# Hybrid decoder block: written instruction order replaced by list scheduling on four engines in the input projection

## The chip, the cores and the metric

The kernel runs on one core of a Trainium2 chip. A core has five engines with instruction streams of their own: TensorE (PE, matmuls and transposes, with its weight loads listed apart as PEld), VectorE (DVE), ScalarE (ACT), GpSimd (POOL) and SyncE (SP, which here only issues DMAs). Each engine works through its own list of instructions; between engines, semaphores make one wait for another. The metric is the device time of one execution in microseconds (us).

## The reference

One layer of a decoder on 2048 positions of width 1024, all in float32. The input projection is the part that this change touches:

```python
mod = silu(c) @ w_ada + b_ada                  # shift, scale, gate for mixer and FFN
h = rms_norm(x) * (1 + scale1) + shift1
p = h @ w_in                                   # (2048, 3088), split into the columns of three groups
q_a, k_a, v_a = ...                            # attention, 8 heads x 64; q_a, k_a are rms-normed per head
q_m, k_m, v_m, o_m, i_m, f_m = ...             # mLSTM, 4 heads x 64, chunk recurrence over 64 positions
u_s, v_s = ...                                 # spatial gating, 4 groups x 64, chunks of 128 positions
y = concat(attention, sigmoid(o_m) * rms_norm(mlstm), gelu(u_s) * spatial(layer_norm(gelu(v_s)))) @ w_out
x = x + gate1 * y
x = x + gate2 * conv_ffn(rms_norm(x) * (1 + scale2) + shift2)
```

## The kernel before

Each float32 matrix product is done as three matmuls on two halves of each operand (`mm3`, L53 to L56): a high part (`hh` of h, `wh` of the weight) and the rest (`hl`, `wl`); the product of the two rests is left out. PE has three places for a product in progress (`acc`), two of them in the last V step.

The projection takes about the first 770 us. It runs in 14 steps (`steps`, L1136): a half of the positions (eight row tiles of 128) times a block of weight columns. Blocks are KM with the gates (272 columns), QO (512, transposed output), VM (256), U and S of the gating (512), K, Q and V (512 each). A row tile of a step is 24 matmuls, 8 slices of 128 in depth (k) times three, into one `acc`; then it is evicted by ACT and DVE. K and Q tiles are normed on the way: ACT squares (`qsq`, L836), DVE sums (`ss`, L841, L842), POOL takes the power -1/2 (L128), DVE multiplies (`qn`, L846), PE transposes (L850), and ACT and DVE split the result into `qhi` and `qlo` (L854, L855), which SP writes to `q_d` or `k_d` (L857). V tiles go through `vhl` (L829, L830) to `v_d` (L831).

Between the tiles side work is interleaved. `slot()` (L463) is called after a tile (and within some), and lets each waiting "lane", a Python generator, do one piece: the weight loads `wr` (L632, L640) and casts `wh` (ACT, L652) and `wl` (DVE, L653) of the next step, which `products` (L682) spreads over the tiles; the rest of the modulation (`wa` loads L486, multiplications L500 and L502 into `modacc`, the bias row L517, the sum over partitions on PE L521 or L527); the mLSTM chunks and, at each quarter's end, `mlstm_end` (L1067) with its sum L1082, L1083, the power on POOL L1084 and the product L1086; norm and transposes of the next rows of x (L559 to L571, L605, L609 to L611, where `xt` is a normed row tile); and in the last step the first rows of scores (L206 to L223) of attention head 0, with their loads of `kk`, `nf` and `q` (L157, L158, L173).

The framework has two ways to order instructions. By default a list scheduler puts each engine's instructions into an order of its own making, from its model of their durations and their dependencies. Inside `tc.manual_schedule(engines=...)` the named engines keep the order in which the Python code writes the instructions. The first step (`first_block`, L1146) is outside; steps 1 to 13 are inside, for PE, DVE, ACT and POOL. SP is never named, so the DMA issues are always ordered by the scheduler. Behind the projection both programs are the same.

Of the kernel before, what the change touches and what calls it, by code (L numbers as in the profile page):

```python
# [33 lines left out]
def trunk(  # L34
# [103 lines left out]
    def attention_open_right():  # L138
        pool.open("att_s", "right", ("nm", 8, 6), ("rs", 8, 6))
        pool.open("att_r", "right", ("kvA", 8192, 3), ("LA", 4096, 8), ("qA", 2048, 4))  # L140
        pp.open("att_r", "right", ("sp", 4096, 2))
# [9 lines left out]
    def load_k(h):  # L151
        tag, e = "kvA" if h == 0 else "kvB", slice(h % 2 * 64, h % 2 * 64 + 64)
        kk = pool.tile([P, S], F32R, name="kk", tag=tag)
        nf = pool.tile([P, S], F32, name="nf", tag=tag)
        vv = pool.tile([P, S // P, P], F32R, name="vv", tag=tag)
        for i in range(2):
            dma(kk[64 * i : 64 * i + 64].bitcast(F32), k_d[h // 2, i, e])  # L157
        dma(nf, nf_d[h : h + 1, :].broadcast_to([P, S]))  # L158
        kv[h] = kk, nf, vv

    def load_v(h, cs):
        for c in cs:
            dma(
                kv[h][2][:, 4 * c : 4 * c + 4].bitcast(F32),
                v_d[c * TB : (c + 1) * TB, h, :].rearrange("(n p) d -> p n d", p=P),
            )

    def load_q(h, tb, tag):
        q2 = []
        for n in range(2):  # L170
            t = pool.tile([P, TB], F32R, name="q", tag=tag)
            for i in range(2):
                dma(  # L173
                    t[64 * i : 64 * i + 64].bitcast(F32),
                    q_d[h // 2, n, h % 2 * 64 : h % 2 * 64 + 64, tb * TB : (tb + 1) * TB],
                )
            q2.append(t)
        return q2
# [281 lines left out]
    def lane(steps_, delay=1, own=False, heavy=False):  # L460
        lanes.append([now[0] + delay, steps_, own, heavy])

    def slot(busy=False, drain=False):  # L463
        now[0] += 1
        for ln in list(lanes):
            if drain and ln[2]:
                continue
            if ln[0] <= now[0] and not (busy and ln[3]):
                w = next(ln[1], 0)
                if w == 0:  # L470
                    lanes.remove(ln)
                else:
                    ln[0] = now[0] + (w or 1)
# [62 lines left out]
    def small_setup():  # L536
        rows = []
        for i in range(2):
            r = pool.tile([P, P], F32, name="crow", tag="tmpA")
            if i == 0:  # L540
                dma(r[0:44], w_conv[0, 0].rearrange("(k p) -> k p", p=P))
                dma(r[44:88], w_conv[0, 1].rearrange("(k p) -> k p", p=P))
            else:
                dma(r[0:44], w_conv[0, 2].rearrange("(k p) -> k p", p=P))
                dma(r[44:88], b_conv[0].rearrange("(k p) -> k p", p=P))
            rows.append(r)
        yield 3
        for i, r in enumerate(rows):
            ps = misc_ps()
            T.transpose(ps[:, 0:88], r[0:88, :], ident[0:88, 0:88])  # L550
            V.tensor_copy(colC[:, i * 88 : (i + 1) * 88], ps[:, 0:88])
            yield 1
# [312 lines left out]
    def log_gates():  # L865

        fox, fm = gates[:, :, 64:72], gates[:, :, 32:36]
        mn = pool.tile([P, 8, 12], F32, name="lg0", tag="lg")
        ab = pool.tile([P, 8, 12], F32, name="lg1", tag="lg")
        for sl, g in ((slice(0, 8), fox), (slice(8, 12), fm)):  # L870
            V.tensor_scalar(mn[:, :, sl], g, 0.0, None, op0=ALU.min)
            V.scalar_tensor_tensor(ab[:, :, sl], mn[:, :, sl], 2.0, g, op0=ALU.mult, op1=ALU.subtract)
        A.activation(ab, ab, AF.Exp)
        A.activation(ab, ab, AF.Ln, bias=1.0)
        yield 1
        for sl, g in ((slice(0, 8), fox), (slice(8, 12), fm)):
            V.tensor_tensor(g, mn[:, :, sl], ab[:, :, sl], op=ALU.subtract)
# [232 lines left out]
    def refill():  # L1110
        xs = [load_x(8 + t) for t in range(4)]
        yield 3
        yield from normed(xs)
        for k in range(KT):
            make_h(2, xs, (k,))
            if k not in (4, 6):
                yield 1
        xs = [load_x(12 + t) for t in range(4)]
        yield 4
        yield from normed(xs)  # L1120
        for k in range(0, KT, 2):
            make_h(3, xs, (k, k + 1))
            yield 1
# [60 lines left out]
    def in_turn(*gens):  # L1184
        for g_ in gens:
            yield from g_

    in_order = tc.manual_schedule(
        engines={mybir.EngineType.PE, mybir.EngineType.DVE, mybir.EngineType.Activation, mybir.EngineType.Pool}
    )  # L1190
    for n, (half, i) in enumerate(steps):
        if n == 1:
            in_order.__enter__()
            lane(in_turn(log_gates(), iter((6,)), small_setup()), 2)
            lane(rest_of_mod(), 1)
        if n == 3:
            lane(in_turn(mlstm(0, 2), mlstm(1, 7)), 2, False, True)
        if n == nb - 1:
            lane(refill(), 3)
        if n == nb + 2:  # L1200
            lane(in_turn(log_gates(), iter((1,)), mlstm(2, 1), mlstm(3, 1, 1)), 1, False, True)
        if n == len(steps) - 1:
            assert n_mod[0] == 64, n_mod
            while any(not ln[2] for ln in lanes):
                slot(drain=True)
            n_accs[0] = 2
            pool.close("proj_r")
            pp.close("proj_r")
            attention_open_right()

            load_k(0)
            first_rows = [], []
            first = [scores(0, tb, load_q(0, tb, "qA"), r) for tb, r in zip((1, 0), first_rows)]
            load_v(0, (0, 1))
            lane(in_turn(*first), 7, True)
        light[0] = 2 if n == 1 else int(0 < n and i < 3)
        if n in (1, nb):
            light[1] = now[0] + (23 if n == 1 else 31)
        nxt[0] = Weights(blocks[steps[n + 1][1]][0]) if n + 1 < len(steps) else None
        if n == 0:  # L1220
            first_block()
        else:
            blocks[i][1](half, cur)
        if nxt[0]:
            nxt[0].cast()
        cur = nxt[0]
    in_order.__exit__(None, None, None)
    pool.close("proj_l")
    pp.close("proj_l")

# [624 lines left out]
```

## Time and profile before

| | |
|---|---|
| three runs | 2670.3, 2672.68, 2673.54 us (median 2672.68) |
| profiled execution | 2675.71 us, of which 2674.0 are the span |
| mean granted PE clock of the profiled execution | 0.988 |
| busy: PE, PEld, DVE, ACT, POOL | 2580.6, 2128.9, 1992.1, 1285.4, 415.6 us |
| DMA | 377.52 MB, mean 141 GB/s |

The profile comes from one execution; its times start at the span's start. A row of the timeline gives the start, the busy time, the engine, the line, what is computed from what, and in brackets how long the engine had been idle and what it had been waiting for. The granted clock is the share of full speed that PE was allowed; below 1 every matmul takes longer. Names in the profile are without the numbers that tell the tiles apart; where a number is given below, it comes from the program's order.

### The profile page before, as it was taken

To read this page: it belongs to the slowest core of one execution; us is meant where nothing else is said; L and a number is where in the kernel's file an instruction comes from. 1 tells how busy PE (TensorE), PEld (TensorE's weight loads), DVE (VectorE), ACT (ScalarE), POOL (GpSimd) and SP (SyncE) were. 2 spreads that over 40 slices of the span, in tenths; PEclk is the share of its full clock that TensorE was granted. 3 is DMA by queue.
4 is the path that set the end of the run, shared out by engine and by line. 5 is a ranking of instruction groups with operands and counts; after the bars stand their busy time and mean duration, and the time that the engine had idled before them with its cause. 6 is when DMAs were issued, how large, how long until landed. Compare 5 with 4: busy or idle time off the path is not lost.

```text
span 2674.0 us, 36818 instructions
## 1 busy us (share of the span) xinstructions
PE 2580.6 (97%) x12761; PEld 2128.9 (80%) x12761; DVE 1992.1 (75%) x3432; ACT 1285.4 (48%) x2442; POOL 415.6 (16%) x550
## 2 busy tenths in 40 slices
PE   5899999999899999999999999999999999999999
PEld 5788787888777877777877888888888888888787
DVE  5555656455448888876749888887988887898797
ACT  3333334333248788874436544444444444444443
POOL 4012210022236566640000000000000000000000
PEclk9899999999999999999999999999999999999999
DMA  7533556424554444536742222228222225748533
GB/s 257 154 117 91 150 152 184 132 70 123 138 171 123 115 133 125 136 98 229 276 142 72 90 84 84 82 84 294 89 85 82 84 79 206 267 148 308 177 101 116
DMA packets 297683, 377.52 MB, mean 141 GB/s; under 512 B 31118, under 2 KB 189676, under 8 KB 295448
## 3 DMA queue, kind: packets, MB, share of 16 engines
q1 hardware_dynamic: 297496, 375.16, 44.4%
q8 instruction: 101, 1.65, 0.3%
q14 instruction: 86, 0.70, 0.1%
HBM read 274.34 MB, written 100.74 MB: 140 GB/s over the span
## 4 chain that ended last, share of the span: by engine, by line
PE 74%; DVE 11%; DMA 5%; ACT 4%; issue 4%; POOL 1%; SPq 0%; DVEq 0%; ACTq 0%; POOLq 0%
PE ub L54 10%; PE ub L56 10%; PE ub L55 10%; PE acc L54 5%; PE acc L56 5%; PE acc L55 5%; PE db L55 4%; PE db L56 4%; PE db L54 4%; PE tp L259 3%; PE sp L206 3%; PE op L245 2%; PE op L246 2%; DVE wspl L1599 2%; DMA x_d<-x 1%
## 5 line engine op out<-in xcount | busy, mean ns | idle before, releaser
L54 PE MATMUL acc<-wh,hh 128*128 128x512 f32 (+2 forms) x768 | 290.8, 379 | 10.9 <-DVE vhl L830 5.3
L55 PE MATMUL acc<-wl,hh 128*128 128x512 f32 (+2 forms) x768 | 277.5, 361 | 4.5 <-POOL wl L677 3.4
L54 PE MATMUL ub<-T,wsph 128*128 128x512 f32 x704 | 274.3, 390 | 5.8 <-ACT wsph L1467 5.8
L56 PE MATMUL acc<-wh,hl 128*128 128x512 f32 (+2 forms) x768 | 278.1, 362 | 0.4 <-DVE hl L611 0.4
L56 PE MATMUL ub<-T,wspl 128*128 128x512 f32 x704 | 273.8, 389 | 0.4 <-DVE wspl L1468 0.4
L55 PE MATMUL ub<-T,wsph 128*128 128x512 f32 x704 | 273.9, 389 | 0.0
L55 PE MATMUL db<-wspl,wsph 128*128 128x512 f32 x616 | 240.4, 390 | 2.2 <-DVE wspl L1599 2.2
L56 PE MATMUL db<-wsph,wspl 128*128 128x512 f32 x616 | 239.6, 389 | 0.0
L54 PE MATMUL db<-wsph 128*128 128x512 f32 x616 | 238.3, 389 | 0.3 <-ACT wsph L1598 0.3
L1467 ACT CAST wsph<-S 128x512 fp32r<-128x512 f32 x176 | 109.7, 623 | 228.6 <-PE ub L55 162.5
L263 DVE TENSOR_TENSOR plo<-tp,phi 128x512 fp32r<-128x512 f32 (+1 forms) x320 | 186.8, 607 | 35.9 <-ACT phi L262 34.0
L54 PE MATMUL ub<-B,wsph 128*128 128x512 f32 x528 | 207.3, 393 | 2.6 <-ACT wsph L1467 2.6
L56 PE MATMUL ub<-B,wspl 128*128 128x512 f32 x528 | 207.0, 392 | 0.8 <-DVE wspl L1468 0.8
L55 PE MATMUL ub<-B,wsph 128*128 128x512 f32 x528 | 207.1, 392 | 0.0
L223 ACT ACTIVATE L<-L,nm 128x1024 f32<-128x1024 f32 (+2 forms) x192 | 172.5, 902 | 32.1 <-DVE nm L212 30.8
L259 PE MATMUL tp<-ident,L 128*128 128x128 f32 x1088 | 178.6, 276 | 5.2 <-DVE vhl L830 1.9
L262 ACT CAST phi<-tp 128x512 fp32r<-128x512 f32 (+1 forms) x320 | 160.1, 521 | 46.0 <-PE tp L259 44.7
L54 PEld LDWEIGHTS acc<-wh,hh 128*128 128x128 f32 x768 | 148.3, 193 | 32.3 <-issue 6.6
L206 PE MATMUL sp<-kk,q 128*128 128x512 f32 (+3 forms) x640 | 168.4, 374 | 2.3 <-DVE nm L212 1.2
L228 POOL TENSOR_SCALAR L<-L,rs 128x1024 f32<-128x1024 f32 (+2 forms) x192 | 167.2, 881 | 11.2
L1598 ACT CAST wsph<-act 128x512 fp32r<-128x512 f32 x132 | 82.2, 623 | 179.0 <-PE db L55 162.6
L55 PEld LDWEIGHTS acc<-wl,hh 128*128 128x128 f32 x768 | 148.2, 193 | 25.1 <-POOL wl L677 3.7
(344 smaller groups left out, 6025.8 us busy)
## 6 DMA issues: line engine op xcount, KB each, us to landing
w<-in_w_up_dram SPq DMA_DIRECT2D x88, 512.0 KB
wd<-in_w_down_dram SPq DMA_DIRECT2D x176, 256.0 KB
wa<-in_w_ada_dram SPq DMA_DIRECT2D x96, 256.0 KB
act_d<-yc SPq DMA_DIRECT2D x44, 512.0 KB
act<-act_d SPq DMA_DIRECT2D x44, 512.0 KB
wr<-in_w_in_dram SPq DMA_DIRECT2D x76, 256.0 KB
q<-q_d SPq DMA_DIRECT2D x128, 128.0 KB
hc_d<-hl SPq DMA_DIRECT2D x28, 512.0 KB
```

The lines of the kernel that those rows point to most:

```text
L54: T.matmul(ps, lh, rh, start=start, stop=False, skip_group_check=resume)
L55: T.matmul(ps, lh, rl, start=False, stop=False, skip_group_check=resume)
L56: T.matmul(ps, ll, rh, start=False, stop=stop, skip_group_check=resume)
L206: T.matmul(sp[:, b : b + bw], q2[n][:, qs], kk[:, s0 + b : s0 + b + bw], start=n == 0, stop=n == 1 and not last)
L223: A.activation(L[c], L[c], AF.Exp, bias=nm[:, n - 1 : n], scale=-1.0, accum_out=rs[:, c : c + 1])
L228: G.tensor_scalar(t, t, rs[:, 0:1], 1.0, op0=ALU.mult, op1=ALU.mult)
L245: T.matmul(op[:, c0:], vv[:, j, :], hi[:, c0:], start=(j == 0), stop=False)
L259: T.transpose(tp[:, i * P : (i + 1) * P], rows[i][j // 8][:, (j % 8) * P : (j % 8 + 1) * P], ident)
L262: A.copy(hi[:, c0:], tp[:, c0:])
L263: V.tensor_tensor(lo[:, c0:], tp[:, c0:], hi[:, c0:].bitcast(F32), op=ALU.subtract)
L1467: A.copy(hi, src)
L1598: A.copy(hi, v)
```

## The change

The region in which four engines keep the written order is taken out. From step 1 on the list scheduler now orders PE, DVE, ACT and POOL too, together with the first block and with what follows. No instruction is added, removed or changed on any engine.

```diff
-    in_order = tc.manual_schedule(
-        engines={mybir.EngineType.PE, mybir.EngineType.DVE, mybir.EngineType.Activation, mybir.EngineType.Pool}
-    )
     for n, (half, i) in enumerate(steps):
         if n == 1:
-            in_order.__enter__()
             lane(in_turn(log_gates(), iter((6,)), small_setup()), 2)
             lane(rest_of_mod(), 1)
...
         if nxt[0]:
             nxt[0].cast()
         cur = nxt[0]
-    in_order.__exit__(None, None, None)
     pool.close("proj_l")
     pp.close("proj_l")
```

The order shows some 146 PE, 670 DVE, 79 ACT, 59 POOL and 270 SP instructions at other places, all in the first 780 us or so. Three places are shown. The tile numbers of the changed kernel are two lower, and lines behind L1188 four or five lower.

First, PE in the first block (about 67 to 80 us of the profile), where `trp` are the transposes of the second four row tiles `xt`, one `trp` for each slice k, and `acc_811` (now `acc_809`) is the first product that needs them. Before, the last transposes and the first matmuls behind them:

```order
L605 MATMUL trp_789<-ident_74,xt_570 128x128
L605 MATMUL trp_800<-ident_74,xt_564 128x128
L605 MATMUL trp_800<-ident_74,xt_566 128x128
L605 MATMUL trp_800<-ident_74,xt_568 128x128
L605 MATMUL trp_800<-ident_74,xt_570 128x128
L54 MATMUL acc_811<-wh_346,hh_729 128x272
L55 MATMUL acc_811<-wl_347,hh_729 128x272
L56 MATMUL acc_811<-wh_346,hl_730 128x272
```

And in the changed kernel, where the transposes of slice 2 and 3 begin:

```order
L605 MATMUL trp_743<-ident_74,xt_562 128x128
L605 MATMUL trp_743<-ident_74,xt_564 128x128
L605 MATMUL trp_743<-ident_74,xt_566 128x128
L605 MATMUL trp_743<-ident_74,xt_568 128x128
L54 MATMUL acc_809<-wh_346,hh_727 128x272
L55 MATMUL acc_809<-wl_347,hh_727 128x272
L605 MATMUL trp_754<-ident_74,xt_562 128x128
L605 MATMUL trp_754<-ident_74,xt_564 128x128
L605 MATMUL trp_754<-ident_74,xt_566 128x128
L605 MATMUL trp_754<-ident_74,xt_568 128x128
L56 MATMUL acc_809<-wh_346,hl_728 128x272
L54 MATMUL acc_846<-wh_346,hh_727 128x272
```

The matmuls of the first slices, of several products at once, moved in between the transposes of the later slices.

Second, DVE at the end of the first half's K step (about 287 to 299 us), where `wl` are the casts of the Q weights and H and `mss` belong to the end of an mLSTM quarter. Before:

```order
L1075 TENSOR_TENSOR H_1861<-H_1861,den_2701 128x16x64
L846 TENSOR_TENSOR qn_2712<-acc_2584,ss_2659 128x512
L653 TENSOR_TENSOR wl_2719<-wr_2556,wh_2718 128x512
L653 TENSOR_TENSOR wl_2728<-wr_2619,wh_2727 128x512
L653 TENSOR_TENSOR wl_2737<-wr_2681,wh_2736 128x512
L841 TENSOR_REDUCE ss_2743<-qsq_2675 128x8
L842 TENSOR_SCALAR ss_2743<-ss_2743 128x8
L653 TENSOR_TENSOR wl_2754<-wr_2722,wh_2753 128x512
L855 SCALAR_TENSOR_TENSOR qlo_2771<-trp_2765,colA_87,qhi_2770 128x512
L846 TENSOR_TENSOR qn_2776<-acc_2643,ss_2743 128x512
L653 TENSOR_TENSOR wl_2779<-wr_2731,wh_2778 128x512
```

And after:

```order
L653 TENSOR_TENSOR wl_2735<-wr_2679,wh_2734 128x512
L842 TENSOR_SCALAR ss_2741<-ss_2741 128x8
L941 TENSOR_TENSOR decr_2794<-mprev_2626,ra_2619 4x4
L943 SCALAR_TENSOR_TENSOR fr_2796<-ones_83,fc_1799,mps_2621 8x512
L846 TENSOR_TENSOR qn_2774<-acc_2641,ss_2741 128x512
L947 COPY fc_2798<-fr_2796 8x1
L1083 TENSOR_SCALAR mss_2803<-mss_2803 128x16
L927 COPY mprev_4854<-mcar_297 4x1
L1086 TENSOR_TENSOR hq_2708<-H_1859,mss_2803 128x1024
L653 TENSOR_TENSOR wl_2752<-wr_2720,wh_2751 128x512
L855 SCALAR_TENSOR_TENSOR qlo_2769<-trp_2763,colA_87,qhi_2768 128x512
L653 TENSOR_TENSOR wl_2777<-wr_2729,wh_2776 128x512
```

The two last casts, `wl_2752` and `wl_2777`, now stand behind L1083 and L1086, between which POOL's L1084 has to be done; `qn_2710` (before `qn_2712`) moved ahead of L1075, out of this piece.

Third, SP at the end of the projection (about 704 to 723 us): `wr` are the loads of the V weights, `kk`, `nf` and `q` the loads for the scores of head 0. Before:

```order
L857 DMA q_d_60<-qhi_6736 128x4x128
L640 DMA wr_6721<-in_w_in_dram 128x512
L1095 DMA yt_d_68<-yt_6728 128x512
L857 DMA q_d_60<-qlo_6737 128x4x128
L640 DMA wr_6752<-in_w_in_dram 128x512
L640 DMA wr_6761<-in_w_in_dram 128x512
L857 DMA q_d_60<-qhi_6800 128x4x128
L857 DMA q_d_60<-qlo_6801 128x4x128
L857 DMA q_d_60<-qhi_6867 128x4x128
L857 DMA q_d_60<-qlo_6868 128x4x128
L157 DMA kk_6829<-k_d_61 64x2048 x2
L158 DMA nf_6830<-nf_d_63 128x2048
```

And after:

```order
L857 DMA q_d_60<-qhi_6734 128x4x128
L1095 DMA yt_d_68<-yt_6726 128x512
L857 DMA q_d_60<-qlo_6735 128x4x128
L640 DMA wr_6750<-in_w_in_dram 128x512
L640 DMA wr_6759<-in_w_in_dram 128x512
L157 DMA kk_6827<-k_d_61 64x2048
L857 DMA q_d_60<-qhi_6798 128x4x128
L857 DMA q_d_60<-qlo_6799 128x4x128
L157 DMA kk_6827<-k_d_61 64x2048
L158 DMA nf_6828<-nf_d_63 128x2048
L173 DMA q_6833<-q_d_60 64x512 x2
L173 DMA q_6836<-q_d_60 64x512 x2
```

The load `wr_6719` (before `wr_6721`) is no longer in this piece; it is a dozen rows earlier. The loads of head 0 moved ahead of the last writes to `q_d` and of the writes of `vhl` to `v_d`. On PE the first six score rows of head 0 (L206, L210), which stood one by one between halves of the V products, are now one group ahead of `acc_6974`.

## Prediction

> **What bounds the kernel now.** I read the page's totals first, then the windows of 25 us, then the timeline of TensorE (PE), which puts the idle time before a group in brackets with what ended it.
>
> ```profile
> span 2674.0 us, 36818 instructions
> PE 2580.6 (97%) x12761; PEld 2128.9 (80%) x12761; DVE 1992.1 (75%) x3432; ACT 1285.4 (48%) x2442; POOL 415.6 (16%) x550
> PEclk9899999999999999999999999999999999999999
> ```
>
> PE is busy for 97% of the span, and both programs hold the same PE instructions. An order can therefore give or take only PE's idle time and time at a low granted clock. Both lie early:
>
> ```profile
> 50.00:75.00 25.00, 19.55 (x107) 17.14 (x106) 11.49 (x37) 12.22 (x28) 3.50 (x8) 0.77 0.28 95
> 100.00:125.00 25.00, 25.00 (x104) 20.48 (x104) 12.00 (x20) 6.80 (x9) 0.00 (x0) 0.90 0.76 232
> 275.00:300.00 25.00, 21.49 (x93) 16.63 (x92) 18.50 (x33) 10.62 (x18) 3.27 (x2) 0.93 0.65 192
> 500.00:525.00 25.00, 22.64 (x156) 20.34 (x155) 16.79 (x35) 9.09 (x16) 0.00 (x0) 0.93 0.46 128
> 600.00:625.00 25.00, 24.04 (x133) 19.83 (x132) 17.96 (x41) 11.33 (x21) 9.77 (x6) 1.00 0.31 92
> 700.00:725.00 25.00, 18.06 (x75) 14.30 (x74) 12.35 (x23) 7.08 (x13) 4.91 (x3) 0.86 0.54 146
> 725.00:750.00 25.00, 21.54 (x93) 17.37 (x92) 4.55 (x11) 3.53 (x9) 0.00 (x0) 0.93 0.77 222
> ```
>
> The columns are width, busy time and count of PE, PEld, DVE, ACT, POOL, then granted clock, DMA share, GB/s. A clock of 0.86 over 25 us is 3.5 us of missing PE work; 0.93 is 1.75 us; 0.90 is 2.5 us. The order differs only up to about 780 us, so nothing later is counted. The PE waits in that stretch that the sum uses:
>
> ```profile
> 66.79 0.33 PE L605 MATMUL trp<-ident,xt 128*128 128x128 f32 x1 [0.49 <-DVE xt L571]
> 68.47 0.33 PE L605 MATMUL trp<-ident,xt 128*128 128x128 f32 x1 [1.35 <-DVE xt L571]
> 70.14 0.33 PE L605 MATMUL trp<-ident,xt 128*128 128x128 f32 x1 [1.34 <-DVE xt L571]
> 71.81 1.33 PE L605 MATMUL trp<-ident,xt 128*128 128x128 f32 x5 [1.34 <-DVE xt L571]
> 99.16 0.79 PE L56 MATMUL acc<-hh,wl 128*128 128x512 f32 x1 [2.29 <-DVE wl L653]
> 289.29 0.84 PE L850 MATMUL trp<-ident,qn 128*128 128x128 f32 x4 [2.31 <-DVE qn L846]
> 298.33 0.50 PE L55 MATMUL acc<-wl,hh 128*128 128x512 f32 x1 [0.97 <-DVE wl L653]
> 465.31 1.10 PE L521 MATMUL mp<-modacc,ones 128*128 128x512 f32 x2 [1.71 <-DVE modacc L517]
> 518.24 1.18 PE L521 MATMUL mp<-modacc,ones 128*128 128x512 f32 x1 [2.21 <-DVE modacc L517]
> 714.10 0.76 PE L54 MATMUL acc<-wh,hh 128*128 128x512 f32 x1 [5.06 <-DVE qn L846]
> 739.78 0.47 PE L54 MATMUL acc<-wh,hh 128*128 128x512 f32 x1 [3.46 <-DVE vhl L830]
> ```
>
> All are waits for side work that another engine reached late in its own order. What counts is whether the scheduler's order puts that work earlier, and what it puts late instead.
>
> **The change, part by part.** Nothing is added or removed on any engine; five places differ in a way that PE can feel. Names are those of the changed kernel (before, two higher).
>
> *A, first block.* The 32 transposes of the second four row tiles ran in one piece, between the matmuls of the first four and those of the second:
>
> ```profile
> 66.70:78.70 12.00, 7.77 (x32) 0.72 0.04 13
> 430.20:431.60 1.40, 1.25 (x8) 1.00 0.75 199
> ```
>
> These are PE's transposes (tile trp) in two windows, busy time and clock. Eight of a later block take 1.25 us at full clock, so 32 take 5.0; here they took 11.9, of which 6.9 is waiting and low clock. Now the matmuls of acc_809, acc_846 and acc_883 stand between them. The last row tile still becomes ready only by L571 near 71.8, and the part of the products that needs it can't move, so I take half, 3.5. At 99.16 PE waited 2.29 for a wl cast and then lost 2.5 by the clock, 4.8 together. Three of the next step's weight casts are moved up; PE also asks 3.5 sooner. Half again, 2.5. **A is 6**, between -3 (the moved casts and modulation operations each push the hh/hl casts by one or two DVE operations) and 6.9 + 4.8 = 11.7.
>
> *B, modulation in the QO step.* 37 rather than 30 L500/L502 operations now stand on DVE ahead of the first VM eviction: 7 more at 0.75 us are 5.2. In the row at 100 us DVE is busy 12.0 of 25, so they hide; if wa loads come late, that cover goes. **B is 0.**
>
> *C, K and Q blocks.* The scheduler puts L846 right behind L842 (in 17 of 32 tiles nothing is between, before in none), though POOL's power stands between them, and L1086 almost right behind L1083:
>
> ```profile
> 282.20 1.64 POOL L128 TENSOR_TENSOR ss<-ss,nhalf 128x8 f32<-128x8 f32 x1 [7.53 <-DVE ss L842]
> ...
> 690.25 2.90 POOL L1084 TENSOR_TENSOR mss<-mss,nhalf 128x16 f32<-128x16 f32 x1 [6.21 <-DVE mss L1083]
> ```
> ```profile
> 299.19 1.27 DVE L943 TENSOR_TENSOR_SCAN fr<-ones,fc,mps 8x512 f32<-8x512 f32 x1
> 613.44 1.22 DVE L1086 TENSOR_TENSOR hq<-H,mss 128x1024 f32<-128x1024 f32 x1
> ```
>
> DVE thus stands still 1.64 us per tile and 2.90 at each of four L1086, with weight casts behind it. At 289.29 qn_2710 no longer waits behind L1075: its power is done at 283.8, so the 2.31 goes. But then qn and six operations up to L943 (1.27) take DVE to about 290.5, and behind it stand, by their own rows, qn_2774 0.68, L1083 0.2, POOL 2.90, L1086 1.22, wl_2752 0.7, a qlo 0.74 and wl_2777 0.7, 7.1 in all and a few tenths of handovers: wl_2777 ends near 298, as before (298.3). The 2.31 thus comes back as a wait of about 3.2 for wl in place of 0.97. Elsewhere DVE has the room: at 13 to 15 busy us in 25, four tiles' powers (6.6) fit; at 17.96 (600 us) they do only as long as no L1083 (2.90) comes with them. **C is -2**, between -9 (four places at the price of this one, 3.2 less the 0.97, about 2.25 each) and +3.3 (both waits go).
>
> *D, gate rows (L517, L521).* L517 came late on DVE because its wa loads and multiplications were spread out. They now run in one stream: the last L517 stands 5 DVE rows behind the first VM eviction of the second half (ev_4755), before 35:
>
> ```profile
> 464.49 0.67 DVE L517 TENSOR_TENSOR modacc<-modacc,brow 1x512 f32<-1x512 f32 x1
> 517.42 0.67 DVE L517 TENSOR_TENSOR modacc<-modacc,brow 1x512 f32<-1x512 f32 x1
> ```
>
> The second wait, 2.21, should go, with about half of the 1.75 of its window: 3.0. At the first, 1.71 goes, but eleven multiplications (8.2 us) now stand ahead of wl_4364, and I give 1.2 of it back: 0.5. **D is 3.5**, between 0 and 2.21 + 1.71 + 1.75 = 5.7.
>
> *E, last Q tiles.* The 5.06 came like this:
>
> ```profile
> 704.72 0.74 DVE L855 SCALAR_TENSOR_TENSOR qlo<-trp,gq,qhi 128x512 fp32r<-128x512 f32 x1
> 707.77 0.62 ACT L652 CAST wh<-wr 128x512 fp32r<-128x512 f32 x1 [2.61 <-DMA wr<-in_w_in_dram]
> 708.42 0.69 DVE L653 TENSOR_TENSOR wl<-wr,wh 128x512 fp32r<-128x512 f32 x1 [1.16 <-ACT wh L652]
> 709.03 0.68 DVE L841 TENSOR_REDUCE ss<-qsq 128x8 f32<-128x512 f32 x1
> 713.27 0.68 DVE L846 TENSOR_TENSOR qn<-acc,ss 128x512 f32<-128x512 f32 x1
> ```
>
> L841 stood behind three wl casts, the last of which waited for its load. The loads now are issued a dozen SP rows earlier, and L841 stands ahead of the casts. From the end of qlo (705.46): three casts (2.07), L842 0.2, POOL 1.64, qn 0.68 and some 0.4 of handovers give 710.4, so PE resumes near 710.5 instead of 714.10: 3.6. Of the 3.5 lost by the clock I take 0.9. **E is 4.5**, between 1 (the powers hold up DVE for two tiles more) and 5.06 + 3.5 = 8.6.
>
> *F, front of the attention.* The V evictions waited for buffers whose writes stood on SP behind the loads of head 0:
>
> ```profile
> 738.80 0.37 ACT L829 CAST vhl<-acc 128x256 fp32r<-128x256 f32 x1 [7.56 <-DMA v_d<-vhl]
> 722.05 1.21 SPq L157 DMA_DIRECT2D kk<-k_d  x2
> 723.93 8.71 SPq L173 DMA_DIRECT2D q<-q_d  x8
> 733.93 6.05 SPq L831 DMA_DIRECT2D v_d<-vhl  x4
> ```
>
> SP needed 11.9 us from the first kk to the first write. Now the loads are ahead of the second pair of q_d writes, so they begin near 710 and end near 722, about when the first write is ready, and the 3.46 at 739.78 goes. In return six score rows stand together ahead of acc_6974, and three exponentials ahead of the eviction vhl_6926 on ACT, for which I take back 1.0. The loads issued by 722 leave about ten us before PE, at 744.19 - 2.7 - 3.46 - 3.6 = 734.4, wants the first row. **F is 2.5**, between -3 and 3.46 + 1.75 = 5.2.
>
> Sum: 6 + 0 - 2 + 3.5 + 4.5 + 2.5 = 14.5 us. The profiled execution took 2675.7 (span 2674.0 and 1.7 around it), so 2661.2 on its scale. It was 3.0 above the median of the three runs, 2672.7; on their scale I forecast **2658**.
>
> *A page against the rows.* Much of A, D and E is clock. The window with the 2.21 us wait has a clock of 0.93, the stretch after the 2.29 one 0.90. The Trainium skill, "TensorE: Matmul & The Clock Gate", section "What's actually happening", has the clock drop only after an idle window of about 3.4 us. By that rule neither of these waits should cost clock, and the sum would be about 11 rather than 14.5. The rows disagree with it, and I go by them.
>
> **The rivals.**
> *No change that can be told* (0.2%, 5.3 us, is about what a measurement of this kernel tells from none). C reaches its end of -9 and A only 2: 2 - 9 + 3.5 + 4.5 + 2.5 = 3.5, so 2669. For it: the new wl wait at 298 comes out of the order itself. Against: at the other three L1086 no cast that PE wants soon is close behind.
> *Slower: DVE becomes the bound in K and Q.* Each of 32 tiles waits 1.64 for POOL on an engine that takes its instructions in order; all exposed, that is 52.5. It decides where DVE's own work passes some 16 us in 25, since four tiles add 6.6 and L1083 2.9: the windows at 275 (18.50) and 600 (17.96) do. With half exposed, 26 in place of the 2, the sum is -9.5 and the time 2682. Against: between them DVE is at 12 to 15.
> *More*: all of A, D, E and F's waits go, with their clock: 11.7 - 2 + 5.7 + 8.6 + 5.2 = 29, so 2643; a little short of that, 2646.
> That the change does nothing is excluded: some 670 DVE and 270 SP instructions stand elsewhere.
>
> **How the numbers follow.** Forecast 0.47, more 0.12, no change 0.23, slower 0.18. The forecast's own range is 2650 to 2667, all of it over 5.3 us faster; with the larger gain that is 0.59 for faster, 0.23 within, 0.18 slower. The range reaches over the larger gain down to 2643, and up to the middle of the slower case, 2682, to leave out no more than 2 in 10.
>
> **What would show it.** A: transposes spread over the acc matmuls and no wait near 95; E and F: no PE wait above 2 us between 700 and 745; D: L517 done before PE's L521; C: DVE idle for POOL in each Q tile, PE waiting for wl near 296. The forecast is wrong if PE shows new waits for wl, qn or trp in K and Q that add up to over 10 us, or if the score rows wait for kk, nf or q.

## The result and the profile after

| | before | after |
|---|---|---|
| median of the runs | 2673.11 us (4 runs, 2670.3 to 2675.19) | 2649.84 us (4 runs, 2646.43 to 2651.47) |
| ratio, 95% interval | | 0.9912 [0.9895, 0.9929] |
| profiled execution | 2675.71 us (span 2674.0) | 2651.47 us (span 2649.8) |
| mean granted clock in it | 0.988 | 0.991 |

The list order is 23 us faster (0.9%). The forecast was 2658, 14.5 faster; the time lies inside the stated range, 0.2 us below the 2650 to 2667 that the prediction called the forecast's own, on the side of the larger gain.

The first lines of the page of the kernel after (span; busy time and share of each engine; granted clock in 40 slices):

```profile
span 2649.8 us, 36811 instructions
PE 2567.2 (97%) x12745; PEld 2125.4 (80%) x12761; DVE 1986.6 (75%) x3432; ACT 1287.7 (49%) x2442; POOL 414.2 (16%) x550
PEclk8999999999999999999999999999999999999999
```

The busy times of DVE, ACT and POOL are those of before within 6 us. PE is busy 13.4 us less for the same work: 7.7 of them because less of it ran at half clock, and some because 16 of its records are missing from this trace. The rest of the 24 us is idle time of PE. The windows of 25 us after (columns as before: busy time and count of PE, PEld, DVE, ACT, POOL, then granted clock, DMA share, GB/s):

```profile
50.00:75.00 25.00, 21.04 (x136) 19.87 (x137) 17.68 (x49) 14.42 (x29) 1.78 (x4) 0.80 0.45 149
100.00:125.00 25.00, 25.00 (x120) 20.57 (x119) 14.50 (x25) 3.68 (x5) 0.00 (x0) 1.00 0.74 243
275.00:300.00 25.00, 20.16 (x93) 15.45 (x93) 12.73 (x25) 9.08 (x20) 10.03 (x7) 0.93 0.53 154
450.00:475.00 25.00, 22.77 (x165) 22.11 (x164) 7.21 (x23) 5.49 (x13) 0.00 (x0) 0.93 0.53 149
500.00:525.00 25.00, 25.00 (x138) 20.32 (x139) 8.86 (x23) 14.19 (x26) 4.44 (x6) 1.00 0.25 69
700.00:725.00 25.00, 22.45 (x98) 17.94 (x99) 8.25 (x20) 7.29 (x18) 7.50 (x12) 0.93 0.67 206
725.00:750.00 25.00, 24.10 (x108) 19.30 (x106) 4.90 (x13) 4.88 (x13) 2.77 (x5) 1.00 0.27 95
```

PE is busier at 50, 500, 700 and 725 us, and less so at 275. The waits of PE behind these windows (timeline of PE after, idle time and releaser in brackets):

```profile
65.84 0.44 PE L605 MATMUL trp<-ident,xt 128*128 128x128 f32 x2 [1.12 <-DVE xt L571]
67.04 1.12 PE L605 MATMUL trp<-ident,xt 128*128 128x128 f32 x4 [0.76 <-ACT h L609]
89.74 0.50 PE L56 MATMUL acc<-hh,wl 128*128 128x512 f32 x1 [0.41 <-DVE wl L653]
281.51 0.52 PE L55 MATMUL acc<-wl,hh 128*128 128x512 f32 x1 [4.46 <-DVE wl L653]
414.17 0.33 PE L605 MATMUL trp<-ident,xt 128*128 128x128 f32 x1 [1.39 <-DVE xt L1100]
453.75 0.39 PE L54 MATMUL acc<-wh,hh 128*128 128x272 f32 x1 [2.06 <-ACT wh L652]
692.83 0.47 PE L54 MATMUL acc<-wh,hh 128*128 128x512 f32 x1 [0.80 <-DVE qn L846]
701.04 0.47 PE L54 MATMUL acc<-wh,hh 128*128 128x512 f32 x1 [2.00 <-DVE vhl L830]
720.08 0.50 PE L206 MATMUL sp<-kk,q 128*128 128x256 f32 x2 [1.29 <-DVE nm L212]
758.12 0.53 PE L206 MATMUL sp<-kk,q 128*128 128x512 f32 x2 [2.95 <-DMA q<-q_d]
```

Of the three waits of some 1.3 us for `xt` one is left (1.12). Gone are the 2.29 for `wl` near 99, the 2.31 for `qn` near 289, both waits for `modacc`, the 3.46 for `vhl` near 740, and nearly all of the 5.06. New are 4.46, 1.39, 2.06, 1.29 and 2.95, and outside these rows 1.89 at 53.11 (for ACT's `h`) and 1.44 at 602.80 (for ACT's `evq`).

The projection can be cut at the ends of product tiles that both kernels have. The table gives the time between two such ends, from the traces. The stages are named by the time of their ends in the profile of before. Beside before and after stand three runs of the experiments: e1, whose order turned out to be that of before; e11, which is before but for one product moved to another engine, and no faster; and e6, which is after with one kind of write on another queue, and no faster. They show how far a stage varies from one execution to the next.

| stage, us of before | before | e1 | e11 | after | e6 | term |
|---|---|---|---|---|---|---|
| 0 to 91.2 (first block) | 91.2 | 90.7 | 91.3 | 83.6 | 84.6 | A |
| to 108.0 | 16.8 | 15.4 | 13.5 | 12.1 | 11.8 | A |
| to 140.5 | 32.5 | 32.5 | 30.9 | 29.6 | 29.9 | B |
| to 281.1 | 140.6 | 140.6 | 140.5 | 140.5 | 140.5 | |
| to 416.3 | 135.2 | 134.1 | 134.6 | 132.6 | 133.0 | C |
| to 452.3 | 36.0 | 36.0 | 36.0 | 38.8 | 35.7 | C |
| to 472.9 | 20.7 | 20.6 | 20.5 | 23.3 | 23.6 | D, first |
| to 527.6 | 54.6 | 54.5 | 52.9 | 49.8 | 49.8 | D, second |
| to 694.8 | 167.2 | 167.2 | 167.2 | 168.5 | 168.4 | C |
| to 722.8 | 28.1 | 29.1 | 27.9 | 20.2 | 19.2 | E |
| to 774.5 | 51.7 | 52.2 | 51.9 | 50.1 | 49.8 | F |

The mean of the first three less the mean of the last two, added over all stages, is 24 us, beside the 23.3 of the medians. Nothing behind the projection is needed to account for the gain.

**A correction to the text ahead of the prediction.** It says that the first block lies outside the region of the written order. It doesn't: the region begins where `tc.manual_schedule(...)` is called, ahead of the loop, and not at `__enter__()`. In the kernel before, the first block was thus in written order as well. The rows of the order shown there are right; only the reason why they differ was wrong. The first experiment showed this.

### The profile page after: what moved, and what is told of

The parts are those of the page before. It is cut to its first block, busy times and chain, and to the rows that moved or that the text cites. A ratio compares the mean times of both kernels' runs of the same rounds, so it can differ in the third digit from the quotient of the medians.

```text
span 2649.8 us, 36811 instructions
## 1 busy us (share of the span) xinstructions
PE 2567.2 (97%) x12745; PEld 2125.4 (80%) x12761; DVE 1986.6 (75%) x3432; ACT 1287.7 (49%) x2442; POOL 414.2 (16%) x550
## 4 chain that ended last, share of the span: by engine, by line
PE 49%; DVE 6%; DMA 4%; ACT 2%; issue 1%; POOL 0%; SPq 0%; DVEq 0%; ACTq 0%; POOLq 0%
PE ub L56 11%; PE ub L54 11%; PE ub L55 11%; PE db L55 3%; PE db L56 3%; PE db L54 3%; DMA wd<-in_w_down_dram 2%; DVE wspl L1594 2%; PE wps L56 1%; PE wps L54 1%; PE wps L55 1%; PE tp L259 1%; PE sp L206 1%; DMA ld<-in_w_out_dram 1%; DMA ld<-y_d 1%
## 5 line engine op out<-in xcount | busy, mean ns | idle before, releaser
L206 PE MATMUL sp<-kk,q 128*128 128x512 f32 (+3 forms) x640 | 169.0, 375 | 6.7 <-DMA q<-q_d 3.0
```

The lines of the kernel that those rows point to most:

```text
L206: T.matmul(sp[:, b : b + bw], q2[n][:, qs], kk[:, s0 + b : s0 + b + bw], start=n == 0, stop=n == 1 and not last)
```

## The experiments

The diffs of e1, e2, e3, e4, e9, e10 and e11 are read against the changed kernel with the region put back in part; "all four" stands for the four engines of the change. The median of before in the runs shared by e1 to e4 was 2672.13, by e5 to e8 2671.24, by e9 to e12 2670.72.

### Which part of the program brings it

**e1**, meant to free the first block and step 1 alone:

```diff
+    in_order = tc.manual_schedule(engines=all four)
     for n, (half, i) in enumerate(steps):
+        if n == 2:
+            in_order.__enter__()
...
+    in_order.__exit__(None, None, None)
```

> List scheduling for steps 0 and 1 only (first block and the QO step); written order on the four engines from step 2 on. Theory (gains sit at separate places and add up): the lead of the changed kernel over before at the end of the QO step is 15.2 us in the traces, so about 15 us faster than before, 2658, with PE's wait before the QO weights near 90 us at 0.4 and no gap at 135. Rival (the scheduler gains only as a whole, and a boundary between list scheduling and written order costs what it gives): at most 5 us faster, 2668 or more.

2669.8 us, ratio 0.9997 [0.9988, 1.0006]. Neither theory was tested: the order of this kernel is that of before on every engine, since the call, not `__enter__()`, opens the region. What it gives is a second profile of the old order, and a measure of chance: its runs lie between 2668.24 and 2676.99.

**e9**, the same question put rightly, with call and enter together at step 2:

```diff
+        if n == 2:
+            in_order = tc.manual_schedule(engines=all four)
+            in_order.__enter__()
...
+    in_order.__exit__(None, None, None)
```

> e1 turned out to have exactly the order of before: the region of written order begins where tc.manual_schedule is called, not where it is entered, and e1 had that call in front of the loop. Here the call itself stands at step 2, so the first block and the QO step are list scheduled (their PE order is that of the changed kernel) and steps 2 to 13 are in written order. Theory (places add up): the lead over before is 12 to 15 us at the end of the QO step and stays there to the end: 2657 to 2660. Rival (the gain of the first block is eaten at the border to the written order): under 6, 2666 or more.

2660.7 us, 0.9956 [0.9943, 0.997]: 10 us, or 12 by the ratio, about half of the whole gain, from the first block and step 1. Its first three stages are 84.5, 11.8 and 29.5, as after.

**e2**, only the last two steps (Q and V of the second half) freed:

```diff
+    in_order = tc.manual_schedule(engines=all four)
     for n, (half, i) in enumerate(steps):
+        if n == 12:
+            in_order.__exit__(None, None, None)
         if n == 1:
+            in_order.__enter__()
```

> Written order for steps 1 to 11, list scheduling for the last two (Q and V of the second half). Theory: terms E and F alone, 17.0 to 25.4 us of lead in the traces, less about 1 given back in the attention: about 7 us faster than before, 2666; the PE wait of 5.06 at 714 shrinks below 2. Rival (the end gains only because the wr loads were moved by the steps before it): under 3 us, 2671 or more, and the 5.06 stays above 3.

2662.98 us, 0.9968 [0.9955, 0.9981], some 9 us, a little more than expected. The stage to 722.8 takes 20.2 here, as after: E needs nothing of what is done earlier.

**e3**, meant to free steps 2 to 11 alone:

```diff
+        if n == 2:
+            in_order.__exit__(None, None, None)
+        if n in (1, 12):
+            in_order = tc.manual_schedule(engines=all four)
+            in_order.__enter__()
...
+    in_order.__exit__(None, None, None)
```

> Written order for step 1 and for the last two steps, list scheduling for steps 2 to 11. Theory: the lead goes from 15.2 to 17.0 over these steps, so 2 us faster than before, 2671: new waits (wl near 281 and wh near 454 in the changed kernel) take back nearly all that the waits at 289 and 518 gave. Rival (the middle is where the scheduler does harm, its entry into written order at Q costs more): 2675 or more. Rival (the middle gains much once the rest is as before): 2665 or less.

2656.65 us, 0.9945 [0.9933, 0.9957]: a miss by 14 us, for the reason found with e1. The first block was freed with it (84.6 in its first stage). What A brought is in this time; step 1 was in written order here, and its stage takes 31.0, so that B isn't.

**e10**, the list order at both ends and the written order in steps 2 to 11:

```diff
+        if n == 2:
+            in_order = tc.manual_schedule(engines=all four)
+            in_order.__enter__()
+        if n == 12:
+            in_order.__exit__(None, None, None)
```

> Written order for steps 2 to 11 only (called at step 2, left at step 12); first block, QO, and the last two steps list scheduled. Theory (gains add up: 12 to 15 in front, about 0 to 1 in the middle, 11 at the end as in e2): 2645 to 2648, thus 2 to 5 us under the changed kernel, whose middle gave 1.8 us in all. Rival (the middle under list scheduling is needed for the front or the end): 2655 or more.

2652.51 us, 0.9924 [0.9912, 0.9936], some 4 us or more above what was expected, and not told from after (0.9912). Over steps 2 to 11 the written order is therefore as good as the list order, within what these runs can tell. So C and D together are worth about nothing; e5 shows why.

### Which engine's order

**e4**, PE alone in written order, from the start to the end of the projection:

```diff
+    in_order = tc.manual_schedule(engines={mybir.EngineType.PE})
     for n, (half, i) in enumerate(steps):
         if n == 1:
+            in_order.__enter__()
...
+    in_order.__exit__(None, None, None)
```

> PE alone keeps the written order from step 1 on, DVE, ACT and POOL are list scheduled. Theory (PE's own order gives only the mixing of transposes and matmuls in the first block, 7.6 us, and the score rows in front; the rest is side work on the other engines): 2650 if the first block's PE order stays mixed, up to 2658 if it does not. Rival (PE's order is what gains): near before, 2668 or more.

2653.96 us, 0.9933 [0.992, 0.9945]. With PE's order untouched, 18 of the 23 us are still there, so most of the gain is made on the engines that PE waits for. PE's own list order works both ways: against after, e4 takes 6.2 us more in its first three stages and 3.6 less in the last (46.5).

**e8**, as after, but PE's order written in the first block:

```diff
+        if n == 0:
+            pe_order = tc.manual_schedule(engines={mybir.EngineType.PE})
+            pe_order.__enter__()
         if n == 1:
+            pe_order.__exit__(None, None, None)
```

> The changed kernel with PE alone in the written order in the first block (step 0), everything else list scheduled. Theory (half or more of the first block's 12.2 us lead is the mixing of the second transposes with matmuls on PE): the lead at the end of the first block's products falls from 7.6 to 3 or less, total 4 to 7 us over the changed kernel, 2655. Rival (the lead comes from DVE, ACT and SP being early; PE's order only follows): 2651 or less.

2653.07 us, 0.9928 [0.9915, 0.9941]: 3.2 over after by the medians, 4.3 by the ratios. The first stage takes 86.7, against 83.6 and 84.6 (after, e6) and 91.2 before. In e4, whose order on PE, DVE and ACT is the same as here through this stage, it takes 88.5; a stretch of half clock at 78.11, which e8 doesn't have, makes most of the difference. So the transposes mixed among PE's matmuls are worth 2.6 to 4.4 us of the 7.0, and the order of the other engines, with the norms of x earlier on DVE and ACT, the rest. Which of the two is the larger isn't settled by these two profiles. The theory's lead of 3 or less was missed (4.5), and so was the rival's 2651 or less.

**e7**, as after, but PE's order written in steps 12 and 13:

```diff
+        if n == 12:
+            pe_order = tc.manual_schedule(engines={mybir.EngineType.PE})
+            pe_order.__enter__()
...
+    pe_order.__exit__(None, None, None)
```

> The changed kernel with PE alone in the written order for the last two steps, so that the score rows of head 0 stand one by one between halves of the V products again. Theory (the group of six score rows ahead of acc_6974 gives back part of what the loads ahead of the V writes gain; with PE written the lead rises by 5.2 from the first V tile to the last, with the group by 1.6): 2 to 4 us under the changed kernel, 2647. Rival (the first rows are not what costs, the wait of 2.95 for q at 758 only comes earlier): same as the changed kernel within 1 us.

2646.05 us, 0.9906 [0.989, 0.9921]: 3.8 under after by the medians, as expected, but 1.6 by the ratios, and the intervals overlap. Its last stage takes 46.5, against 50.1 after and 51.7 before; 24 matmuls of score rows fall into this stage in all of them. In the changed kernel six rows stand together ahead of a V product and bring a wait of 1.29 us at 720 (for L212 on DVE), which is gone in e7. Not all of the 3.6 us is their place: after has a stretch of half clock in this stage that costs 1.7, and e7 has none. In e2 and e10, which have the group of six and no half clock there, the stage takes 48.4 and 48.5, so the place alone is worth some 2 us. Whether it also brings the half clock isn't shown.

### POOL's power between two DVE instructions

Of the new waits the longest is the 4.46 at 281.51. DVE and POOL ahead of it, in the timeline of the kernel after:

```profile
276.46 0.15 DVE L1083 TENSOR_SCALAR mss<-mss 128x16 f32<-128x16 f32 x1
...
276.70 2.90 POOL L1084 TENSOR_TENSOR mss<-mss,nhalf 128x16 f32<-128x16 f32 x1 [0.94 <-DVE mss L1083]
...
279.63 1.23 DVE L1086 TENSOR_TENSOR hq<-H,mss 128x1024 f32<-128x1024 f32 x1 [2.83 <-POOL mss L1084]
280.77 0.68 DVE L653 TENSOR_TENSOR wl<-wr,wh 128x512 fp32r<-128x512 f32 x1
```

DVE stands still 2.83 us for POOL, multiplies for 1.23, and only then casts the `wl` that PE has been waiting for. It is the wait that term C told, with its cause and in its place.

**e5**, as after, with L1086 on POOL itself, so that DVE needn't wait:

```diff
-        V.tensor_tensor(hq, hn, bc(ss, 3, 64), op=ALU.mult)
+        G.tensor_tensor(hq, hn, bc(ss, 3, 64), op=ALU.mult)
```

> The changed kernel with the product L1086 (hq times mss, four times) on POOL, right behind the power L1084 there, instead of on DVE. PE's order is the same. Theory (the 4.46 us PE wait for wl at 281.5 comes from DVE standing still for POOL's 2.9 us and then doing L1086 with the casts behind it): that wait falls by at least 2.9, to 1.5 or less, DVE's 2.83 us idle before L1086 is gone, and the lead over before at the third tile of the Q step rises from 14.4 to 17 or more; total about 3 us under the changed kernel, 2647. Rival (the casts are late because the weight loads are): the wait stays near 4.

2639.32 us, 0.9879 [0.9866, 0.9893]: 10.5 us under after by the medians and 8.8 by the ratios, about three times what was expected. At the first place, in the timeline of this kernel:

```profile
277.40 2.90 POOL L1084 TENSOR_TENSOR mss<-mss,nhalf 128x16 f32<-128x16 f32 x1 [0.93 <-DVE mss L1083]
277.52 0.69 DVE L653 TENSOR_TENSOR wl<-wr,wh 128x512 fp32r<-128x512 f32 x1
...
280.12 0.50 PE L55 MATMUL acc<-wl,hh 128*128 128x512 f32 x1 [0.67 <-DVE wl L653]
...
280.37 2.14 POOL L1086 TENSOR_TENSOR hq<-H,mss 128x1024 f32<-128x1024 f32 x1
```

The cast starts while POOL still computes the power; PE's wait falls from 4.46 to 0.67. The stage to 416.3 takes 129.1, against 132.6 and 133.0. The surprise is the stage to 472.9: 19.0, against 23.3 and 23.6. The 2.06 at 453.75 is gone too, though it is a wait for a `wh` cast on ACT. Its history, in the timeline of the kernel after (SPq is SP's queue of DMA issues):

```profile
433.27 3.34 POOL L1084 TENSOR_TENSOR mss<-mss,nhalf 128x16 f32<-128x16 f32 x1 [20.13 <-DVE mss L1083]
...
436.64 1.23 DVE L1086 TENSOR_TENSOR hq<-H,mss 128x1024 f32<-128x1024 f32 x1 [2.80 <-POOL mss L1084]
...
438.39 1.52 DVE L502 SCALAR_TENSOR_TENSOR modacc<-wa,cs,modacc 128x512 f32<-128x512 f32 x2
...
440.99 3.13 SPq L486 DMA_DIRECT2D wa<-in_w_ada_dram  x5
...
447.04 1.54 DVE L502 SCALAR_TENSOR_TENSOR modacc<-wa,cs,modacc 128x512 f32<-128x512 f32 x2 [1.18 <-DMA wa<-in_w_ada_dram]
...
449.28 0.78 DVE L653 TENSOR_TENSOR wl<-wr,wh 128x272 fp32r<-128x272 f32 x2
...
449.81 1.82 SPq L640 DMA_DIRECT2D wr<-in_w_in_dram  x4
...
453.27 0.42 ACT L652 CAST wh<-wr 128x272 fp32r<-128x272 f32 x1 [7.90 <-DMA wr<-in_w_in_dram]
```

Behind the waiting L1086 stood the multiplications L502. They free the `wa` buffers, so the next `wa` loads were issued later, and the later L502, which need those loads, ran later too. Behind them in DVE's order stand two `wl` casts. The first of them frees a `wr` buffer; the `wr` load is issued 0.1 us after it ends, the `wh` cast on ACT waits for the load, and PE for the cast. In e5 the same stretch of DVE and POOL reads:

```profile
427.59 3.34 POOL L1084 TENSOR_TENSOR mss<-mss,nhalf 128x16 f32<-128x16 f32 x1 [18.60 <-DVE mss L1083]
428.71 2.31 DVE L502 SCALAR_TENSOR_TENSOR modacc<-wa,cs,modacc 128x512 f32<-128x512 f32 x3
```

L502 runs while POOL works, the `wr` load is issued 14.0 us after L1083 instead of 16.8, and PE waits nowhere near. An engine with room to spare, held for 2.80 us and then by 1.23 us of product, thus cost PE a wait 17 us later, by way of two kinds of buffer that it freed late.

**e6**, as after, to tell what holds that `wr` load: the `yt_d` writes (L1095), one of which stands right ahead of it on SP, are issued on ACT's queue.

```diff
-            dma(yt_d[512 + j * P : 640 + j * P, t0 : t0 + 512], yt)
+            nc.scalar.dma_start(out=yt_d[512 + j * P : 640 + j * P, t0 : t0 + 512], in_=yt)
```

> The changed kernel with the writes of yt (L1095) issued from ACT's queue instead of SP's. Theory (the 2.06 us PE wait for wh at 453.75 comes from the weight loads that stand on SP behind the write of yt, which waits for DVE): the loads are issued 2 us or more earlier, the wait goes, and with it the half clock behind it, 2.6 us in all; 2647. Rival (the loads are held by the modulation loads ahead of them on SP, whose buffers the multiplications free): the wait stays within 0.5 of 2.06.

2647.86 us, 0.9911 [0.9898, 0.9924]; the wait is still 1.87 us. The write wasn't the cause. The rival is right that the wait stays, but what held the load directly was not the `wa` loads, the last of which SP issued at 441.75. SP's own waits from 440 to 453 us of this kernel (total, times, longest) name a `wl` cast on DVE:

```profile
SPq L640 <- DVE wl L653: 6.5, 2, 6.1
```

The load is issued at 448.38, as the first of two casts that began at 447.92 ends. That this cast came late because of L1086 is what e5 shows.

**e11**, the same edit on the kernel before:

```diff
-        V.tensor_tensor(hq, hn, bc(ss, 3, 64), op=ALU.mult)
+        G.tensor_tensor(hq, hn, bc(ss, 3, 64), op=ALU.mult)
```

> The kernel before, all in written order, with only the product L1086 on POOL. Theory (L1086 hurts only where the scheduler puts it right behind the power with weight casts behind it): within 3 us of before, 2669 to 2675; the wait of 2.31 at 289 stays, since it comes from L1075. Rival (taking 1.22 us four times off DVE and onto POOL gains in any order): 2664 or less.

2669.26 us, 0.9995 [0.9986, 1.0005]: nothing, as expected. In the written order other work stood between L1083 and L1086, and DVE stood still before only one of the four products, in the timeline of before:

```profile
455.86 1.23 DVE L1086 TENSOR_TENSOR hq<-H,mss 128x1024 f32<-128x1024 f32 x1 [1.54 <-POOL mss L1084]
```

In the changed kernel it stood still before all four, 9.4 us together. The 9 to 10 us that e5 gains are thus a cost that the list order brought, not one that the kernel had.

**e12**, e5 and e7 together:

```diff
-        V.tensor_tensor(hq, hn, bc(ss, 3, 64), op=ALU.mult)
+        G.tensor_tensor(hq, hn, bc(ss, 3, 64), op=ALU.mult)
...
+        if n == 12:
+            pe_order = tc.manual_schedule(engines={mybir.EngineType.PE})
+            pe_order.__enter__()
...
+    pe_order.__exit__(None, None, None)
```

> The changed kernel with L1086 on POOL and PE in written order for the last two steps. Theory (the two gains, 10.5 and 3.8 us, are at different places and add up): 2635 to 2637. Rival (the second is covered by the first, since the V evictions come at another time): 2639.

2638.46 us, 0.9875 [0.9861, 0.9888], not told from e5 alone (2639.32). Its last stage is 46.7, so e7's gain is there, but the stage to 694.8 takes 169.5 instead of 167.4, of which a stretch of half clock at 634.63 is 1.7. Of the versions run, these two are the fastest, 1.2% under the kernel before.

## Why the prediction was right in its direction and short in size

The sum was 14.5, the stages give 24, between the forecast and the rival in which all of A, D, E and F goes (29). Forecast against the means of the table:

**A, first block: 6 forecast, 10 measured** (7.0 in the first stage, 3.3 in the second). The mechanism was right: no wait above 0.41 near 90 us, transposes spread over the products. Mis-sized was the step "the last row tile still becomes ready only by L571 near 71.8, so I take half". The row tiles themselves come earlier, since DVE's and ACT's order in the first block changed too: the last wait for `xt` in the kernel after ends at 65.84. By e8 and e4 this is 2.6 to 4.4 us of the 7.0 in the first stage. The prediction looked at PE's order there and not at DVE's.

**B, modulation in the QO step: 0 forecast, 2 measured.** The added multiplications do hide. Not counted was a wait that went; in the timeline of before:

```profile
134.99 1.05 PE L527 MATMUL mp<-ones,modacc 128*128 128x1 f32 x8 [1.37 <-DVE colC L551]
```

It and the half clock behind it (in e11 there was none) are the 1.2 to 2.8 us by which the stage was longer than in after and e6. It stands in the same timeline of PE that the prediction read, and the prediction doesn't name it.

**C, K and Q blocks: -2 forecast, -0.6 measured** (+1.8, -1.2 and -1.2 in its three stages; the second comes from after's profile alone, 38.8 against 35.7 in e6: the 1.39 at 414.17, with the clock behind it, isn't in e6, e7 or e8). The size came out by two errors that offset each other. With e5, the five stages from 281 to 695 give 11 us over the old order; with the standstill at L1086 they give 0.7. The new order is thus much better than told there, and its one flaw costs 9 to 10, not 2 (1.3 of the difference is the chance of the second stage). The step that failed is "at the other three L1086 no cast that PE wants soon is close behind": at 436 there was none directly behind, but the multiplications that free the `wa` buffers were, and behind these the casts that free the buffers of the next weight loads. The price of the power in each Q and K tile was rightly seen as hidden; the groups by line, before and then after:

```profile
L846 DVE TENSOR_TENSOR qn<-acc,ss 128x512 f32<-128x512 f32 x32 | 21.8, 682 | 7.6 <-POOL ss L128 7.5
```
```profile
L846 DVE TENSOR_TENSOR qn<-acc,ss 128x512 f32<-128x512 f32 x32 | 22.1, 691 | 41.8 <-POOL ss L128 41.8
```

DVE stands still 41.8 us for POOL, 34 more than before, and PE there has no wait for `qn` above 0.80. This was the rival by which DVE would become the bound, and it fell: DVE has that room.

**D, gate rows: first 0.5 forecast, -2.9 measured; second 3.0 forecast, 4.2 measured.** Both waits for `modacc` went as told. What the first brought was taken back by the 2.06 at 453.75 and the clock behind it, through the chain told under e5 and e6; with e5 this stage is 1.6 us better than before.

**E, last Q tiles: 4.5 forecast, 8.7 measured.** The chain runs as the prediction laid it out, in the timeline of the kernel after:

```profile
687.55 0.74 DVE L855 SCALAR_TENSOR_TENSOR qlo<-trp,gq,qhi 128x512 fp32r<-128x512 f32 x1
688.21 1.89 DVE L653 TENSOR_TENSOR wl<-wr,wh 128x512 fp32r<-128x512 f32 x3
690.01 0.17 DVE L842 TENSOR_SCALAR ss<-ss 128x8 f32<-128x8 f32 x1
690.32 1.64 POOL L128 TENSOR_TENSOR ss<-ss,nhalf 128x8 f32<-128x8 f32 x1 [7.24 <-DVE ss L842]
691.99 0.69 DVE L846 TENSOR_TENSOR qn<-acc,ss 128x512 f32<-128x512 f32 x1 [1.82 <-POOL ss L128]
```

From the end of `qlo` to PE's start at 692.83 it takes 4.5 us; the prediction worked out 5.0. Mis-sized was the clock, and with it the idle time: the waits of 4.91 to 5.82 us were followed by 5.5 to 6.2 us of half clock in each of the three profiles of the old order, and with 0.80 of wait left none of it comes back. Of the 7.9 us between before and after in this stage, 5.1 are idle time (4.3 of them this wait, where the prediction took 3.6) and 2.8 are PE's work at half clock. The prediction had read 3.5 lost by the clock from its window and took 0.9 of them. The 3.5 was itself too much, because the mean clock of a window also counts half clock at which PE stood idle.

**F, front of the attention: 2.5 forecast, 2.0 measured**, and some of it is returned at 758.12, where PE waits 2.95 for `q`. The reason is SP's queue, after:

```profile
737.99 13.23 SPq L831 DMA_DIRECT2D v_d<-vhl  x6
752.68 0.37 SPq L163 DMA_DIRECT2D vv<-v_d  x1
753.15 5.63 SPq L173 DMA_DIRECT2D q<-q_d  x8
```

These `q` loads stand behind six V writes that were held up. The prediction named such a wait among what would make it wrong, and priced nothing for it.

**The clock.** The prediction counted the half clock behind waits of 2.2 and 2.3 us as a fixed price. It isn't one. The same 2.29 us wait near 99 us, in the same order, was followed by 6.1 us of half clock in before and 3.4 in e1, so it cost 3.0 and 1.7 us of PE's work; in e11 it cost none. The timeline of e11, then its window:

```profile
98.87 0.50 PE L56 MATMUL acc<-hh,wl 128*128 128x512 f32 x1 [2.29 <-DVE wl L653]
```
```profile
100.00:125.00 25.00, 25.00 (x116) 20.82 (x115) 13.40 (x22) 7.32 (x11) 0.00 (x0) 1.00 0.76 242
```

The window of before has 0.90 there, so some of what the pair of profiles shows for A is chance of the profiled execution of before.

## What to carry to other kernels

A list scheduler that places an instruction right behind the one whose result another engine has still to work on makes an in-order engine stand still. The standstill is free until something that another queue needs (here a buffer's release) lies behind it. So follow what stands behind the waiting instruction through the buffers that it frees to the next loads, not only to the next operand of the bound engine; moving the waiting instruction to the engine that makes its operand removed this cost for nothing. When a written order and a list order are compared, compare each engine's order, and the reach of the region, first.

## What the runs showed of the hardware

How the clock answers a wait of PE, from the clock records of all fourteen traces. Within one trace every change of the granted clock between 60 and 790 us lies on a grid of 3.41 us: of 62 stretches of half clock 50 lasted 3.41 us and 12 twice that. Where PE is busy throughout, 3.41 us of half clock take 1.7 us of its work. Where the grid lies against the program differs from one execution to the next.

What comes next goes with how long PE was busy within one cell of the grid, that is, within 3.41 us between two of its points. Of the cells at full clock, all 44 in which PE was busy for less than 0.44 of the time were followed by half clock, 17 of 45 between 0.44 and 0.60, and one of 2818 above that (0.89, at 631.22 in e12; the cause of this one is open). The same wait of 2.21 us at the second L521, in before and then in e11 (two cells each; columns as in the windows above, the first busy time being PE's, and the clock the third number from the end):

```profile
514.84:518.26 3.42, 1.21 (x11) 1.04 (x10) 2.61 (x6) 2.18 (x4) 0.00 (x0) 1.00 0.31 105
518.26:521.67 3.41, 3.41 (x6) 2.09 (x7) 1.37 (x3) 1.34 (x2) 0.00 (x0) 0.50 0.75 189
```
```profile
510.70:514.12 3.42, 1.54 (x5) 1.01 (x6) 2.81 (x5) 1.87 (x4) 0.00 (x0) 1.00 0.41 122
514.12:517.53 3.41, 3.41 (x20) 2.81 (x19) 0.20 (x3) 2.02 (x4) 0.00 (x0) 1.00 0.71 198
```

In before the whole wait falls into one cell and PE is busy for 1.21 of 3.42 us; half clock follows. In e11 the grid cuts the wait, PE is busy for 1.54 us, and the clock stays full. So behind all fourteen waits of 3.46 to 5.82 us between 60 and 790 us the clock was half, and behind shorter ones it depends on how the grid happens to cut them. The 2.29 near 99 us was followed by half clock in before and e1, and by full clock in e2 and e11. A wait of 2.00 for `vhl` was followed by it in after, e5 and e8, and not in e2, e4, e7, e10 and e12. In the kernel after, 1.39 us at 414.17 was enough (with other short waits in its cell PE was busy for 1.68 of 3.41 us), and 2.95 at 758.12, cut in two, was not.

The Trainium skill, "TensorE: Matmul & The Clock Gate", section "What's actually happening", has the clock fall to half behind an idle window of some 3.4 us, and says that this window runs freely. The two values, the length of the window and its free running agree with these traces. That the window has to be idle doesn't agree with them: cells in which PE was busy for up to 0.60 of the time were followed by half clock, so that 3.4 us is no bound below which a wait costs nothing.

And the chance is large beside the effects that were studied: e11, one program, was timed between 2661.69 and 2675.35 us, wider than its difference from before by far. That is why stages are compared here over several profiles.
